# Operands of the down projection by row tiles, their remainders on VectorE, block sums moved ahead, and both halves' output projections ended token tile by token tile

## The chip, the core and the metric

The kernel runs on one NeuronCore of a Trainium2 chip. The metric is the device time of one execution in microseconds (us); lower is better. TensorE (PE) multiplies 128x128 blocks into PSUM. VectorE (DVE), ScalarE (ACT) and GpSimd (POOL) work element by element, and SyncE (SP) issues nearly all transfers between the memory outside (DRAM) and SBUF. All five run their own instruction streams and wait for each other by semaphores.

## The reference

One encoder layer on x (1024 tokens, 1024 columns, float32). Cut to what the change touches:

```python
merged = jax.nn.sigmoid(gate_a) * ya + jax.nn.sigmoid(gate_b) * yb      # two attentions before it
x = x + jnp.einsum("bsd,de->bse", merged, w_o[i])                       # output projection
h2 = rmsnorm(x, g_mlp[i])
u = jax.nn.relu(jnp.einsum("bsd,df->bsf", h2, w_up[i]))                 # 1024 -> 4096
x = x + jnp.einsum("bsf,fd->bsd", u * u, w_down[i])                     # 4096 -> 1024
h3 = rmsnorm(x, g_ple[i])
gate = jax.nn.sigmoid(jnp.einsum("bsd,de->bse", h3, w_ple_gate[i]))
x = x + gate * jnp.einsum("bsk,kd->bsd", p[i], w_ple[i])                # p: 1024 tokens, 256 columns
return rmsnorm(x, g_final)
```

The kernel keeps float32 accuracy.

## The kernel before

**A product in float32.** Each operand is split into a rounded part (fp32r, `hi`) and a remainder (`lo` = value minus `hi`), and each block product is three matmuls: hi·hi, hi·lo and lo·hi (`mm3`, L119 to L126). So each operand costs one cast (mostly ACT) and one subtraction (DVE or POOL) before PE can use it. Nearly all matmuls stand on L126.

**The stages in order.** The input projection with its gates (to about 240 us of the trace), two attentions (to 700), the merge, the output projection `wo` (766 to 861), the up projection `u` (to 1188), the down projection `d` (1188 to 1534), and the last stage: the gate product `pg`, the product `pp` of p with w_ple, and the final norm (to 1672). The 1024 tokens are worked in two halves of four tiles of 128 tokens (s).

**The order of work.** The program is written per engine as straight code. A scheduler of the framework then puts the instructions of each engine in an order, by its own model of the time; slots of a pool (a `tag` with a number of `bufs`) tie a new tile to the end of use of an older one. The order below is what it gives; each engine executes its list in that order.

**Gate stage.** For each of 16 column tiles d and for each half, `gate` loads 512 KB of w_in (`raw_g`), casts it on ACT (`hi_g`, L103), takes the remainder on DVE (`lo_g`, L105), runs 24 matmuls of 128x512 and stores the sigmoid (`gst`) to DRAM with a DMA on SP.

**Output projection.** `wo(h, n, s)` is 24 matmuls of 128x256 for the half h, the column quarter n and the token tile s. For half 0 all sixteen run first; x_rows(1, s) loads the second half, and then `upper_rows(s)` normalizes the first half's rows, sends them through a transposing DMA (`nhl` to `nt`) and leaves the transposed rows in `R`, from which the operand `H_b` is cut (L839, L840). For half 1, n = 2 and 3 already end tile by tile, and `lower_rows(s)` (L174, L864, L868, L873 to L881) normalizes and transposes on PE (`nt_mlp`) and cuts the up projection's operands `H_t`.

**Down projection.** A seven-product scheme (as Strassen's) on 2x2 blocks: four chunks c of the 4096 rows, and in each seven products i in the order 1, 2, 5, 6, 3, 7, 4 (`run`). A product has an operand from u (`ua`, read back from DRAM, 512 KB each half) and one from w_down (`wd`, in SBUF), each [128, 4, 512]; it multiplies them for four token tiles s: 48 matmuls of 128x512. It is done in two halves `sub_` of two k tiles each. `operand` (L1109 to L1113) makes [P, 2, 2, 512]: the cast on ACT (L1111, 128x1024), the remainder on POOL for `da` and on DVE for `db` (L1112, 128x1024). There are four tags, da0, db0, da1 and db1, with one buffer each, so the cast of the next product's da0 waits until PE has read this product's. Between the products `minus` (L1197, DVE) makes the sums of w_down blocks in place. Products are added to accumulators E[1] to E[7] in SBUF (`put`: L1139 ACT for the first, L1141 DVE after that).

**End of the down projection.** In the last chunk, `sums` (L1071 to L1080) combines the accumulators of half 0 into x, `norm3` (L1086 to L1092) normalizes rows into `xn` and transposes them (`nt_ple`, L202) into h3H and h3L. p is loaded, transposed on PE (`ptt`, L1101), and split into `pT` in the middle of the down projection (`p_rows`, after product 3 of chunk 1).

**Last stage.** For each half, each n of four and each s of four: `pg`, 24 matmuls of 128x256, and `pp`, six of 128x256. `quad` loads and splits w_ple_gate in two parts (`lo_pg`, POOL, L105). The sums of half 1 stand at n = 1 of half 0, and the norms of half 1's tiles 0, 1 and 2, and 3 at n = 1, 2 and 3.

## Time and profile before

| what | value |
|---|---|
| median of 3 runs | 1672.77 us (1672.07 to 1676.2) |
| the profiled execution's own time | 1674.16 us |
| its span, first to last instruction | 1672.4 us |
| TensorE busy, share of the span | 1558.0 us, 93% |
| VectorE / ScalarE / GpSimd busy | 1212.9 / 791.9 / 778.6 us |
| mean granted TensorE clock | 0.979 |

Durations and waits below come from the profiled execution, which is 1.4 us above the median. A wait of an engine costs time only where that engine's work sets the end. TensorE is busy for 93% of the span, so its waits are where a change of order can win time, and the other engines count where TensorE waits for them.

### The profile page before, as it was taken

What the parts mean: (1) busy time and instruction counts of PE and PEld (TensorE: products, weight loads), DVE (VectorE), ACT (ScalarE), POOL (GpSimd) and SP (SyncE); (2) the same over time, 40 slices, a digit from 0 to 9 for tenths busy, and PEclk for the clock granted to TensorE, in tenths of its full rate; (3) what the DMA queues carried; (4) which work ended last, traced back from release to release, by engine and by line L of the source; (5) the groups of instructions that cost most, each with busy time, mean ns of one, the idle gap of its engine ahead of it and who ended that gap; (6) DMA issues with size and microseconds to landing.
All of it is one profiled execution on the core that took longest, in us unless ns stands there. A gap on an engine that the chain in (4) does not pass through costs nothing.

```text
span 1672.4 us, 23829 instructions
## 1 busy us (share of the span) xinstructions
PE 1558.0 (93%) x8514; PEld 1319.1 (79%) x8514; DVE 1212.9 (73%) x1815; ACT 791.9 (47%) x1450; POOL 778.6 (47%) x478
## 2 busy tenths in 40 slices
PE   7999999999899887999987999999999989987978
PEld 7998887777777665789985888888787778766978
DVE  7278238668889878545588999999867767888443
ACT  6344348678898777423443222222343333333533
POOL 4254006547777778322353333333544434465743
PEclk9999999999999999999997999999999999999989
DMA  6023549979999999846634544445944443312331
GB/s 228 26 51 110 148 133 187 226 164 215 203 199 190 194 187 196 223 144 214 177 108 138 173 142 151 159 150 183 383 168 135 135 167 113 127 38 63 116 109 67
DMA packets 435814, 260.96 MB, mean 156 GB/s; under 512 B 284392, under 2 KB 381808, under 8 KB 435312
## 3 DMA queue, kind: packets, MB, share of 16 engines
q1 hardware_dynamic: 434416, 257.34, 59.3%
q10 hardware_dynamic: 1280, 2.10, 0.6%
q8 instruction: 67, 1.10, 0.3%
q14 instruction: 51, 0.42, 0.1%
HBM read 141.89 MB, written 48.30 MB: 114 GB/s over the span
## 4 chain that ended last, share of the span: by engine, by line
PE 57%; DVE 12%; DMA 11%; issue 8%; POOL 7%; ACT 4%; SPq 1%; POOLq 0%; ACTq 0%; DVEq 0%
PE u L126 17%; PE d L126 8%; PE gt L126 8%; DMA PT<-hl 7%; PE pg L126 5%; PE y L126 4%; POOL da L1112 3%; PE z_qb L126 3%; PE wo L126 3%; POOL hl L585 2%; PE av L755 2%; DVE db L1112 1%; PE z_k L126 1%; PE pp L126 1%; DVE p L574 1%
## 5 line engine op out<-in xcount | busy, mean ns | idle before, releaser
L585 POOL TENSOR_TENSOR hl<-p,hl 128x1024 f16<-128x1024 f32 x128 | 278.9, 2186 | 183.4 <-PE gt L126 69.8
L126 PE MATMUL d<-db,da 128*128 128x512 f32 x1344 | 316.7, 396 | 26.4 <-DVE db L1112 19.1
L126 PEld LDWEIGHTS d<-db,da 128*128 128x128 f32 x1344 | 255.2, 191 | 85.6 <-DVE db L1112 27.0
L1112 POOL TENSOR_TENSOR da<-ua,da 128x1024 fp32r<-128x1024 f32 x56 | 144.2, 2575 | 163.8 <-ACT da L1111 160.8
L126 PE MATMUL u<-H_t,wop 128*128 128x512 f32 x768 | 182.5, 394 | 8.5 <-ACT H_t L876 8.5
L126 PEld LDWEIGHTS u<-H_t,wop 128*128 128x128 f32 x768 | 146.1, 191 | 39.9 <-ACT H_t L876 8.9
L574 DVE TENSOR_SCALAR_CACHE_REDUCE p<-s 128x1024 f32<-128x1024 f32 x128 | 155.5, 1217 | 11.4 <-PE s L126 5.4
L1112 DVE TENSOR_TENSOR db<-wd,db 128x1024 fp32r<-128x1024 f32 x55 | 112.4, 2043 | 64.8 <-ACT db L1111 64.8
L577 ACT ACTIVATE p<-p,mx 128x1024 f32<-128x1024 f32 x128 | 147.3, 1151 | 8.9 <-DVE Va L458 1.5
L1111 ACT CAST da<-ua 128x1024 fp32r<-128x1024 f32 x56 | 58.9, 1052 | 187.6 <-issue 162.6
L126 PE MATMUL u<-H_b,wop 128*128 128x512 f32 x576 | 138.4, 394 | 4.3 <-ACT wop L798 4.3
L126 PEld LDWEIGHTS u<-H_b,wop 128*128 128x128 f32 x576 | 109.2, 190 | 27.4 <-ACT wop L798 4.7
L584 DVE TENSOR_SCALAR_CACHE_REDUCE hl<-p 128x512 f16<-128x512 f32 x128 | 87.2, 681 | 49.3 <-DMA PT<-hl 33.3
L1032 POOL TENSOR_TENSOR us<-uq 128x512 f32<-128x512 f32 x15 | 19.7, 1312 | 193.5 <-DVE uq L1028 193.5
L126 PE MATMUL s<-KT,QT 96*128 96x512 f32 x384 | 103.6, 411 | 5.8 <-DVE p L574 5.7
L126 PE MATMUL gt<-hH,hi_g 128*128 128x512 f32 x256 | 100.7, 393 | 2.6 <-ACT hi_g L103 2.6
L126 PE MATMUL gt<-hH,lo_g 128*128 128x512 f32 x256 | 101.4, 396 | 1.7 <-DVE lo_g L105 1.7
L126 PE MATMUL gt<-hL,hi_g 128*128 128x512 f32 x256 | 100.1, 391 | 0.0
L583 ACT CAST hl<-p 128x512 f16<-128x512 f32 x128 | 78.8, 616 | 26.1 <-DMA PT<-hl 23.4
L126 PEld LDWEIGHTS s<-KT,QT 96*128 96x128 f32 x384 | 70.1, 193 | 23.2 <-DVE p L574 7.5
L105 DVE TENSOR_TENSOR lo_g<-raw_g,hi_g 128x1024 fp32r<-128x1024 f32 x32 | 47.6, 1488 | 55.3 <-ACT hi_g L103 55.2
L755 PE MATMUL av<-PT,Va 128*128 128x256 f16 x512 | 66.7, 283 | 20.4 <-DMA PT<-hl 19.4
(331 smaller groups left out, 3867.3 us busy)
## 6 DMA issues: line engine op xcount, KB each, us to landing
ua<-u_d SPq DMA_DIRECT2D x56, 512.0 KB, 3.7
raw_g<-in_w_in_dram SPq DMA_DIRECT2D x32, 512.0 KB, 4.1
raw_up<-in_w_up_dram SPq DMA_DIRECT2D x32, 512.0 KB, 4.6
u_d<-us SPq DMA_DIRECT2D x64, 256.0 KB, 2.0
wd<-in_w_down_dram SPq DMA_DIRECT2D x16, 1024.0 KB, 5.8
u_d<-uq SPq DMA_DIRECT2D x48, 256.0 KB, 2.0
gates_d<-gst SPq DMA_DIRECT2D x32, 256.0 KB, 2.9
gg<-gates_d SPq DMA_DIRECT2D x16, 512.0 KB, 3.3
```

What stands on the lines that cost most here:

```text
L105: eng.tensor_tensor(lo, raw, hi.bitcast(F32), ALU.subtract)
L126: return [pe.matmul(ps, a, b, start=start and i == 0, stop=stop and i == len(m) - 1) for i, (a, b) in list(enumerate(m))[first:last]]
L574: dve.tensor_scalar(e, ps, 1.0, 3e38, op0=ALU.mult, op1=ALU.min, accum_out=mx)
L577: act.activation(e, e, AF.Exp, bias=mx, scale=-1.0, accum_out=sums[:, hd, qt:qt + 1])
L583: act.copy(hl[:, 0, :CUT], e[:, :CUT])
L584: dve.tensor_scalar(hl[:, 0, CUT:], e[:, CUT:], 1.0, 0.0, op0=ALU.mult, op1=ALU.max, accum_out=top)
L585: pool.tensor_tensor(hl[:, 1], e, hl[:, 0], ALU.subtract)
L755: pe.matmul(av[:, :256], values(hd, kt), PT[(2 * g + half) % 3][:, n, kt], start=(kt + n == 0), stop=(kt + n == NS))
L1032: eng.tensor_tensor(v[1], q[:, 2], q[:, 3], ALU.add)
L1111: act.copy(t[:, 0], raw)
L1112: eng.tensor_tensor(t[:, 1], raw, t[:, 0].bitcast(F32), ALU.subtract)
```

## The change

Six edits. (1) `p_rows` runs in the gate stage, at d = 13 and 15, and stores the transposed p to DRAM (`p_d`, eight DMAs of 128 KB through one buffer); at the end of chunk 0 of the down projection it is read back as two loads and split into `pT`. (2) In half 0 of the output projection n = 2 and 3 end tile by tile, with `upper_rows(s)` right behind each. (3) The down operands are made per k tile, [P, 2, 512], from one tag with ten buffers; PE multiplies k by k. All remainders are on DVE (except the first two of the first product), and `minus` moves to POOL. (4) The block sums are taken as soon as their parts are there: for half 0 after products 2, 6 and 3 of the last chunk, for half 1 beside the first `pg` products; `xn` of half 0 uses the storage of E[1]. (5) The product of p with w_ple for half 0, n = 0 and 1 (`pp0`), is done at the end of the down projection, as 24 matmuls of 128x512. (6) The norms of half 1 move up: tiles 0 and 1 at n = 1, 2 and 3 at n = 2.

```diff
 
+    p_d = tc.dram_tile([P, 2, S], F32, name="p_d")
...
+    def p_rows(h):
...
+        pr = raw_tile(f"p{h}", [P, 4, PLE])
+        nc.sync.dma_start(pr, p[512 * h:512 * (h + 1), :].rearrange("(s q) c -> q s c", q=P))
+        for s in range(4):
+            pt = bank(f"ptt{h}_{s}")
+            for k in range(2):
+                pe.transpose(pt[:, k * P:(k + 1) * P], pr[:, s, k * P:(k + 1) * P], ident)
+            v = pt[:, :256].rearrange("p (k s) -> p k s", k=2)
+            t = zp.tile([P, 2, P], F32, tag="junk", name=f"pt{h}_{s}", bufs=1)
+            act.copy(t, v)
+            nc.sync.dma_start(p_d[:, :, (4 * h + s) * P:(4 * h + s + 1) * P], t)
+
...
+        if d in (13, 15):
+            p_rows(d // 15)
...
-        for n in range(4):
+        for n in range(2):
             ws = wo_weights(0, n)
             for s in range(4):
                 wo(0, n, s, ws)
+        R0 = big("R0", [P, NK, 512], F32)
+        ws = [wo_weights(0, n) for n in (2, 3)]
+        for n, s in ((2, 0), (3, 0), (2, 1), (3, 1), (2, 2), (2, 3), (3, 2), (3, 3)):
+            wo(0, n, s, ws[n - 2])
+            if n == 3:
+                upper_rows(s)
...
-        R0 = big("R0", [P, NK, 512], F32)
...
-        for s in range(4):
-            upper_rows(s)
...
-         5: acc[3][:, 0], 7: acc[3][:, 1]}
+         5: acc[3][:, 0], 7: acc[3][:, 1], 8: acc[1][:, 1]}
...
 
-    def sums(h, s):
-
-        e = {i: E[i][:, s] for i in E}
-        if h == 0:
-            dve.tensor_tensor(e[2], e[2], e[1], ALU.add)
-            dve.tensor_tensor(e[6], e[6], e[1], ALU.add)
-            pool.tensor_tensor(e[3], e[3], e[5], ALU.add)
-            dve.tensor_tensor(e[3], e[3], e[6], ALU.add)
-        else:
-            x22 = acc[1][:, 1, s]
-            pool.tensor_tensor(x22, x22, e[5], ALU.add)
-            dve.tensor_tensor(e[6], e[6], e[7], ALU.add)
-            dve.tensor_tensor(x22, x22, e[6], ALU.add)
-            dve.tensor_tensor(e[4], e[4], e[6], ALU.add)
-
-    def norm3(q, h, s):
+    def add(eng, i, j, s):
+        return eng.tensor_tensor(E[i][:, s], E[i][:, s], E[j][:, s], ALU.add)
...
+    def norm3(xn, h, s):
...
-        xn = q.tile([P, D], F32, tag="xn3", name=f"xn3_{h}_{s}", bufs=2)
...
 
-    def p_rows(h):
...
-
     na, np_ = [0], [0]
     with tc.tile_pool(name="dp", bufs=1, reuse_waits="tile") as dp:
-        def operand(side, name, raw, eng):
-            t = dp.tile([P, 2, 2, 512], F32R, tag=side, name=f"{side}_{name}")
+        def operand(name, raw, eng):
+            t = dp.tile([P, 2, 512], F32R, tag="d", name=f"d{name}", bufs=10)
             act.copy(t[:, 0], raw)
             eng.tensor_tensor(t[:, 1], raw, t[:, 0].bitcast(F32), ALU.subtract)
             return t
...
 
+            def part(s, k0, k1):
+                sl = slice(s * P, (s + 1) * P)
+                mm3(pss[s], [(a[:, 0, sl], a[:, 1, sl], b[:, 0], b[:, 1]) for a, b in ab[k0:k1]],
+                    start=k0 == 0, stop=k1 == 4)
+
             ab = []
-            for sub_ in range(2):
-                ab.append((operand(f"da{sub_}", f"{i}_{c}", av[sub_], pool),
-                           operand(f"db{sub_}", f"{i}_{c}", bv[:, 2 * sub_:2 * sub_ + 2],
-                                   pool if c + sub_ == 0 and i == 1 else dve)))
+            for k in range(4):
+                eng = pool if c == 0 and i == 1 and k < 2 else dve
+                ab.append((operand(f"a{k}_{i}_{c}", av[k // 2][:, k % 2], eng), operand(f"b{k}_{i}_{c}", bv[:, k], eng)))
                 if whole:
                     continue
                 for s in range(4):
-                    if sub_ == 0:
+                    if k == 0:
                         room(s)
-                    a, b = ab[sub_]
-                    sl = slice(s * P, (s + 1) * P)
-                    mm3(pss[s], [(a[:, 0, k, sl], a[:, 1, k, sl], b[:, 0, k], b[:, 1, k]) for k in range(2)],
-                        start=sub_ == 0, stop=sub_ == 1)
-                    if sub_ == 1:
+                    part(s, k, k + 1)
+                    if k == 3:
                         put(s)
             if whole:
                 yield
                 for s in range(4):
                     room(s)
-                    sl = slice(s * P, (s + 1) * P)
-                    mm3(pss[s], [(a[:, 0, k, sl], a[:, 1, k, sl], b[:, 0, k], b[:, 1, k]) for a, b in ab for k in range(2)])
+                    part(s, 0, 4)
                     put(s)
                     yield
 
...
             def minus(o, a, b):
                 for sub_ in range(2):
                     ks = slice(2 * sub_, 2 * sub_ + 2)
-                    dve.tensor_tensor(o[:, ks], a[:, ks], b[:, ks], ALU.subtract)
+                    pool.tensor_tensor(o[:, ks], a[:, ks], b[:, ks], ALU.subtract)
                 return o
 
             run(1, c, av[0], b11)
+            t1 = minus(b11, b12, b11)
             run(2, c, av[1], b21)
-            t1 = minus(b11, b12, b11)
+            if last:
+                for s in range(4):
+                    add(pool, 2, 1, s)
+                    add(dve, 6, 1, s)
             run(5, c, av[2], t1)
             av += [a_raw(4, c)]
             t2 = minus(t1, b22, t1)
             run(6, c, av[3], t2)
             av += [a_raw(5, c)]
             t4 = minus(b21, b21, t2)
+            if last:
+                for s in range(4):
+                    add(dve, 3, 5, s)
             run(3, c, av[4], b22)
             av += [a_raw(6, c)]
             t3 = minus(b12, b22, b12)
-            if c == 1:
-                pT = big("pT", [P, 2, 2, S])
-                for h in range(2):
-                    p_rows(h)
             if last:
-                for s in range(2):
-                    sums(0, s)
+                for s in range(4):
+                    add(dve, 3, 6, s)
             run(7, c, av[5], t3)
             end = product(4, c, av[6], t4)
             if last:
                 next(end)
-                norms = []
-                for s in range(4):
-                    if s > 1:
-                        sums(0, s)
-                    norms.append(norm3(dp, 0, s))
+                x1 = E[1].rearrange("p (i s) c -> p i (s c)", i=2)
+                norms = [norm3(x1[:, s % 2], 0, s) for s in range(4)]
...
-                for t in norms[2:]:
-                    next(t)
+
+                pp0 = big("pp0", [P, 4, 512], F32)
+                wp = w_tile("wq", w_ple, 0, 2, 0, 512)
+                for s in range(4):
+                    if s % 2 == 0:
+                        next(norms[2 + s // 2])
+                    ps = bank(f"pp0_{s}")
+                    st = slice(s * P, (s + 1) * P)
+                    mm3(ps, [(pT[:, 0, k, st], pT[:, 1, k, st], wp[0][:, k], wp[1][:, k]) for k in range(2)])
+                    act.copy(pp0[:, s], ps)
             for _ in end:
                 pass
+            if c == 0:
+                pT = big("pT", [P, 2, 2, S])
+                for k in range(2):
+                    raw = raw_tile(f"pT{k}", [P, S])
+                    nc.sync.dma_start(raw, p_d[:, k])
+                    act.copy(pT[:, 0, k], raw)
+                    sub(pT[:, 1, k], raw, pT[:, 0, k])
             if not last:
                 wA = wN
 
...
         for n in range(4):
             cs = slice(256 * n, 256 * (n + 1))
             ws = quad(f"pg{h}_{n}", w_ple_gate, 256 * n, eng=pool, **({"pool_": ep, "tag": "z"} if n % 2 else {}))
-            wp = ple_weights(h, n)
+            if h > 0 or n > 1:
+                wp = ple_weights(h, n)
...
-            if h == 0 and n == 1:
-                for s in range(4):
-                    sums(1, s)
             for s in range(4):
...
                 ps = bank(f"pg{h}_{n}_{s}")
-                mm3(ps[:, :256], [(h3H[h][:, k, sl], h3L[h][:, k, sl]) + ws(k) for k in range(NK)])
-                pp = ple_product(h, n, s, wp, bank(f"pp{h}_{n}_{s}"))
+                mm = mm3(ps[:, :256], [(h3H[h][:, k, sl], h3L[h][:, k, sl]) + ws(k) for k in range(NK)])[0]
+                if h + n == 0:
+                    follow(add(dve, 6, 7, s), mm)
+                    follow(add(pool, 8, 5, s), mm)
+                    add(dve, 4, 6, s)
+                    add(dve, 8, 6, s)
+                pp = pp0[:, s, cs] if h == 0 and n < 2 else ple_product(h, n, s, wp, bank(f"pp{h}_{n}_{s}"))
...
             if h == 0 and n > 0:
-                for s in {1: (0,), 2: (1, 2), 3: (3,)}[n]:
-                    for _ in norm3(ep, 1, s):
+                for s in {1: (0, 1), 2: (2, 3), 3: ()}[n]:
+                    for _ in norm3(ep.tile([P, D], F32, tag="xn3", name=f"xn3_1_{s}"), 1, s):
...
 
```

SP in the gate stage, where the loads of weights (`raw_g`) and the stores (`gates_d`) alternate, before:

```order
L97 DMA raw_g_1_2316<-in_w_in_dram 128x8x128
L474 DMA gates_d<-gst_0_2245 128x512
L97 DMA raw_g_1_2350<-in_w_in_dram 128x8x128
L474 DMA gates_d<-gst_0_2279 128x512
L97 DMA raw_g_1_2384<-in_w_in_dram 128x8x128
L474 DMA gates_d<-gst_0_2313 128x512
```
SP at the same place with the change (`p_d` are the stores of the transposed p):

```order
L474 DMA gates_d<-gst_0_2246 128x512
L489 DMA p_d<-pt_0_2254 256x1x128
L481 DMA raw_p_2343<-in_p_dram 128x4x256
L97 DMA raw_g_1_2369<-in_w_in_dram 128x8x128
L489 DMA p_d<-pt_1_2260 256x1x128
L489 DMA p_d<-pt_2_2266 256x1x128
L474 DMA gates_d<-gst_0_2306 128x512
L97 DMA raw_g_1_2403<-in_w_in_dram 128x8x128
```
Up to two stores of p stand between a weight load and the next store of a gate, and the second load of p stands ahead of a weight load.

DVE in a chunk of the down projection (`wd` is the block of w_down, `ua` that of u, `acc` the accumulators, `d` the product in PSUM), before:

```order
L1112 TENSOR_TENSOR db_1_2_12513<-wd_0_11956,db_1_2_12513 128x1024
L1141 TENSOR_TENSOR acc_11440<-acc_11440,d_1_3_12447 128x512
L1197 TENSOR_TENSOR wd_0_11956<-wd_1_12496,wd_0_11956 128x1024
L1112 TENSOR_TENSOR db_1_2_12545<-wd_0_11956,db_1_2_12545 128x1024
L1197 TENSOR_TENSOR wd_1_12496<-wd_1_12496 128x1024
L1197 TENSOR_TENSOR wd_0_11956<-wd_1_12496,wd_0_11956 128x1024
L1197 TENSOR_TENSOR wd_1_12496<-wd_1_12496 128x1024
L1112 TENSOR_TENSOR db_2_2_12577<-wd_0_11956,db_2_2_12577 128x1024
```
DVE in a chunk with the change:

```order
L1106 TENSOR_TENSOR da_5_1_12321<-ua_1_1_12096,da_5_1_12321 128x512
L1106 TENSOR_TENSOR db_5_1_12324<-wd_0_11507,db_5_1_12324 128x512
L1135 TENSOR_TENSOR acc_11491<-acc_11491,d_1_0_12193 128x1024
L1135 TENSOR_TENSOR acc_11491<-acc_11491,d_1_2_12200 128x1024
L1106 TENSOR_TENSOR da_6_1_12349<-ua_1_0_12098,da_6_1_12349 128x512
L1106 TENSOR_TENSOR db_6_1_12352<-wd_0_11507,db_6_1_12352 128x512
L1106 TENSOR_TENSOR da_6_1_12369<-ua_1_0_12098,da_6_1_12369 128x512
L1106 TENSOR_TENSOR db_6_1_12372<-wd_0_11507,db_6_1_12372 128x512
```
The sums of `wd` are gone from DVE; both remainders, `da` and `db`, now stand there in pairs of half the size.

POOL at the end of the down projection (`lo_pg_n_j` is part j of the gate weights of quarter n, `r_ple` a factor of the norm), before:

```order
L1112 TENSOR_TENSOR da_4_3_13433<-ua_3_0_13355,da_4_3_13433 128x1024
L1112 TENSOR_TENSOR da_4_3_13439<-ua_3_1_13357,da_4_3_13439 128x1024
L105 TENSOR_TENSOR lo_pg_0_1_13617<-raw_pg_0_1_13613,hi_pg_0_1_13615 128x1024
L169 TENSOR_TENSOR r_ple_2_13490<-v_ple_2_13488,mhalf 128x1
L169 TENSOR_TENSOR r_ple_3_13540<-v_ple_3_13538,mhalf 128x1
L105 TENSOR_TENSOR lo_wp_0_13623<-raw_wp_0_13619,hi_wp_0_13621 128x512
L105 TENSOR_TENSOR lo_pg_1_0_13787<-raw_pg_1_0_13783,hi_pg_1_0_13785 128x1024
```
POOL at the same place with the change (L1088 are the block sums of half 1):

```order
L169 TENSOR_TENSOR r_ple_3_13889<-v_ple_3_13887,mhalf 128x1
L105 TENSOR_TENSOR lo_pg_1_0_14157<-raw_pg_1_0_14153,hi_pg_1_0_14155 128x1024
L1088 TENSOR_TENSOR acc_11493<-acc_11493,acc_11495 128x512 x2
L105 TENSOR_TENSOR lo_pg_1_1_14163<-raw_pg_1_1_14159,hi_pg_1_1_14161 128x1024
L1088 TENSOR_TENSOR acc_11493<-acc_11493,acc_11495 128x512
L105 TENSOR_TENSOR lo_pg_0_1_14005<-raw_pg_0_1_14001,hi_pg_0_1_14003 128x1024
L1088 TENSOR_TENSOR acc_11493<-acc_11493,acc_11495 128x512
```
The second part of the first quarter's remainder, `lo_pg_0_1`, stood ahead of both parts of the second quarter; now it stands behind them and behind three sums.

## Rows read from the trace of the kernel before

**Rows 1.** the page: busy time of each engine, share of the span, instructions

```profile
PE 1558.0 (93%) x8514; PEld 1319.1 (79%) x8514; DVE 1212.9 (73%) x1815; ACT 791.9 (47%) x1450; POOL 778.6 (47%) x478
```

**Rows 2.** windows of the four down chunks and the last stage

```profile
core 0: us, PE busy (x) PEld busy (x) DVE busy (x) ACT busy (x) POOL busy (x), PEclk, DMA share, GB/s
1187.80:1267.50 79.70, 77.13 (x338) 62.87 (x337) 55.73 (x36) 35.42 (x39) 33.37 (x14) 1.00 0.68 253
1267.50:1354.20 86.70, 80.68 (x354) 65.43 (x353) 62.21 (x53) 30.51 (x36) 34.64 (x14) 0.98 0.43 145
1354.20:1432.50 78.30, 76.79 (x338) 62.90 (x336) 62.32 (x43) 28.06 (x28) 35.01 (x15) 1.00 0.38 123
1432.50:1533.70 101.20, 84.58 (x355) 67.72 (x354) 88.61 (x78) 34.12 (x40) 58.19 (x27) 0.93 0.19 60
1533.70:1672.40 138.70, 121.82 (x1008) 120.97 (x1006) 65.43 (x127) 60.71 (x146) 70.75 (x58) 0.96 0.30 97
```

**Rows 3.** groups of TensorE in the down projection: busy, mean ns, idle before

```profile
L126 PE MATMUL d<-db,da 128*128 128x512 f32 x1344 | 316.7, 396 | 26.4 <-DVE db L1112 19.1 <-DVE pT L77 3.7 <-DVE v_ple L167 2.7
L1101 PE MATMUL ptt<-ident,raw_p 128*128 128x128 f32 x16 | 2.4, 274 | 0.3 <-DMA raw_p<-in_p_dram 0.3
```

**Rows 4.** timeline of TensorE, down: start, duration, idle before and releaser

```profile
1218.81 49.49 PE L126 MATMUL d<-db,da 128*128 128x512 f32 x217 [0.60 <-DVE db L1112]
1466.58 1.65 PE L126 MATMUL d<-db,da 128*128 128x512 f32 x3 [4.46 <-DVE db L1112]
1522.88 0.80 PE L126 MATMUL d<-db,da 128*128 128x512 f32 x1 [7.51 <-DVE db L1112]
```

**Rows 5.** a window behind one such wait, columns as in 2

```profile
1466.60:1470.00 3.40, 3.40 (x8) 2.72 (x9) 3.15 (x5) 0.00 (x0) 0.12 (x1) 0.50 0.50 150
```

**Rows 6.** timelines of VectorE, then GpSimd, in the down projection

```profile
1253.42 2.58 DVE L1112 TENSOR_TENSOR db<-wd,db 128x1024 fp32r<-128x1024 f32 x1 [2.86 <-ACT db L1111]
1267.93 1.21 DVE L1197 TENSOR_TENSOR wd<-wd,wd 128x1024 f32<-128x1024 f32 x1
1252.51 2.40 POOL L1112 TENSOR_TENSOR da<-ua,da 128x1024 fp32r<-128x1024 f32 x1 [3.04 <-ACT da L1111]
```

**Rows 7.** groups of VectorE and GpSimd, down projection

```profile
L1141 DVE TENSOR_TENSOR acc<-acc,d 128x512 f32<-128x512 f32 x47 | 30.2, 676 | 11.2 <-PE d L126 11.2
L1141 DVE TENSOR_TENSOR acc<-acc,d 128x1024 f32<-128x1024 f32 x24 | 28.5, 1207 | 0.0
L1073 POOL TENSOR_TENSOR acc<-acc,acc 128x512 f32<-128x512 f32 x4 | 6.9, 1764 | 0.0
```

**Rows 8.** groups of VectorE in the up projection

```profile
L799 DVE TENSOR_TENSOR wop<-st_s,wop 128x512 fp32r<-128x512 f32 x60 | 67.4, 1123 | 0.0
L799 DVE TENSOR_TENSOR wop<-raw_up,wop 128x512 fp32r<-128x512 f32 x43 | 29.9, 696 | 0.8 <-ACT wop L798 0.8
```

**Rows 9.** timelines, output to up projection: TensorE, then ScalarE

```profile
884.30 7.84 PE L126 MATMUL u<-H_t,wop 128*128 128x512 f32 x24 [8.48 <-ACT H_t L876]
896.42 0.79 PE L126 MATMUL u<-H_b,wop 128*128 128x512 f32 x1 [4.28 <-ACT wop L798]
848.18 1.14 ACT L839 CAST H_b<-R 128x512 fp32r<-128x512 f32 x2 [5.58 <-DVE R L855]
```

**Rows 10.** timeline of ScalarE, gate stage; a DMA of the page

```profile
225.19 1.05 ACT L103 CAST hi_g<-raw_g 128x1024 fp32r<-128x1024 f32 x1 [3.90 <-PE gt L126]
230.63 1.05 ACT L103 CAST hi_g<-raw_g 128x1024 fp32r<-128x1024 f32 x1 [3.89 <-PE gt L126]
u_d<-us SPq DMA_DIRECT2D x64, 256.0 KB, 2.0
```

**Rows 11.** timeline of TensorE in the last stage

```profile
1592.13 0.28 PE L126 MATMUL pp<-hi_wp,pT 128*128 128x256 f32 x1
1592.84 0.28 PE L126 MATMUL pg<-hi_pg,h3H 128*128 128x256 f32 x1
1605.30 1.08 PE L202 MATMUL nt_ple<-ident,xn 128*128 128x128 f32 x4 [8.74 <-DVE xn L1089]
```

More of the change, by code (lines that the diff above doesn't have):

```diff
@@ L1092, in norm3 @@
         yield
-    def p_rows(h):
-        pr = raw_tile(f"p{h}", [P, 4, PLE])
-        nc.sync.dma_start(pr, p[512 * h:512 * (h + 1), :].rearrange("(s q) c -> q s c", q=P))
-        for s in range(4):
-            pt = bank(f"ptt{h}_{s}")
-            for k in range(2):
-                pe.transpose(pt[:, k * P:(k + 1) * P], pr[:, s, k * P:(k + 1) * P], ident)
-            v = pt[:, :256].rearrange("p (k s) -> p k s", k=2)
-            sl = slice((4 * h + s) * P, (4 * h + s + 1) * P)
-            act.copy(pT[:, 0, :, sl], v)
-            sub(pT[:, 1, :, sl], v, pT[:, 0, :, sl])
     na, np_ = [0], [0]
     with tc.tile_pool(name="dp", bufs=1, reuse_waits="tile") as dp:
-        def operand(side, name, raw, eng):
-            t = dp.tile([P, 2, 2, 512], F32R, tag=side, name=f"{side}_{name}")
+        def operand(name, raw, eng):
+            t = dp.tile([P, 2, 512], F32R, tag="d", name=f"d{name}", bufs=10)
             act.copy(t[:, 0], raw)
@@ L1260, in hybrid_block_kernel @@
             ws = quad(f"pg{h}_{n}", w_ple_gate, 256 * n, eng=pool, **({"pool_": ep, "tag": "z"} if n % 2 else {}))
-            wp = ple_weights(h, n)
+            if h > 0 or n > 1:
+                wp = ple_weights(h, n)
             if gfin_b is None:
                 gfin_b = gain(ep, "gfin_b", g_final.unsqueeze(0))
-            if h == 0 and n == 1:
-                for s in range(4):
-                    sums(1, s)
             for s in range(4):
```

## The prediction

> **What bounds the kernel now.** I began with the busy times. TensorE works for 1558.0 of 1672.4 us [rows 1], so what can be won without fewer matmuls is its waits, about 114 us in all, and the slow stretches behind them. The stage windows say where: the four chunks of the down projection take 79.7, 86.7, 78.3 and 101.2 us, 345.9 together, though each multiplies the same number of matmuls, and the clock is down to 0.93 in the last [rows 2]. In a stretch without a wait TensorE starts 217 matmuls within 49.49 us, that is 49.1/216 = 0.227 us each [rows 4]. A chunk has 7 x 48 = 336 of them, 76.4 us, and the four have 305.5. So 345.9 - 305.5 = 40 us of this stage are no needed matmul time.
>
> The groups of TensorE say what ends its waits there: 26.4 us, of which 19.1 end with the remainder `db` on VectorE, 3.7 with `pT` and 2.7 with the norm [rows 3]. The two longest stand in the last chunk, 4.46 and 7.51 us [rows 4]. Each also costs something behind it: at 1466.6, right after such a wait, the granted clock is 0.50, the 1.2 GHz level, for the next 3.4 us [rows 5].
>
> Why `db` is late is read from the timelines of VectorE and GpSimd together. `da` on GpSimd begins at 1252.51 and takes 2.40 us; `db` on VectorE begins at 1253.42 and ends at 1256.00, 2.58 us after its start, though a VectorE operation of the same size without such a neighbour takes 1.21 [rows 6]. The two block each other: the second one waits for the first. In quiet products this fits into the half product that covers it (24 x 0.227 = 5.4 us), since each operand has a single buffer. When sums or norms come in between, as in the last chunk, there is no further cover, and TensorE waits.
>
> **Down operands by row tiles.** Removed: 56 `da` on GpSimd and 55 `db` on VectorE. Added on VectorE: 56 remainders of 128x512 in each chunk. An operation of this form and size takes 0.696 us for one operand of the up projection and 1.123 for another [rows 8]; I read the longer mean as the price where GpSimd runs beside it often. I take 0.70, since GpSimd now has only the eight sums of w_down blocks in a chunk: 56 x 0.70 = 39 us. Adding products to the accumulators: 30.2 + 28.5 = 58.7 us for 24 products [rows 7], 2.45 each, 17 in a chunk. Together 56 us on VectorE against 76.4 on TensorE. GpSimd's eight sums cost 8 x 2.40 = 19 us, at the price of `da` [rows 6]. If every one of them stopped VectorE for its whole length, 56 + 19 = 75 us: still just under TensorE's 76.4. Also, ten buffers hold five pairs; one pair feeds TensorE for 12 x 0.227 = 2.7 us, so up to four pairs, 10.9 us, lie ahead of it. A VectorE delay of the size seen here (7.51 at most) is then covered. So the waits for `db` go, and the half-clock stretches behind them.
>
> The Trainium skill bears on this: its page "SBUF — State Buffer", section "Who interferes with whom", says that the port pair that VectorE and GpSimd share is an exclusive lock, so that a VectorE operation with two inputs in SBUF and a GpSimd operation that reads SBUF run one after the other. The pair above agrees (1.21 alone, 2.58 beside a `da`). By the rule a chunk's VectorE and GpSimd work simply add, to the 75 us just worked out; so the rule alone doesn't deny the gain, but it leaves next to no reserve and makes the last chunk the place to look.
>
> In the last chunk come 12 VectorE and 4 GpSimd sums (12 x 0.70 = 8.4; 4 x 1.76 = 7 [rows 7]), four norm products (1.2 each, 5), four `h3L` (0.70 each, 3), and two to four remainders of gate weights on GpSimd (2.40 each, 5 to 10). VectorE 56 + 16 = 72; with GpSimd 19 + 7 + 7 = 33 the serial sum is 105 us against about 80 for TensorE. Part of it (the later sums and weights) may lie behind the last product, and most of VectorE's time need not meet GpSimd's; I take 4 us of waits, bounds 0 and 25.
>
> The sum for the stage: 305.5 for matmuls, 1.7 for 16 transposes of the norm (a `ptt` transpose of the same form is busy for 2.4/16 = 0.15 [rows 3]; 0.11 by starts is my estimate), 3 at the start of the first chunk and 1 at each of three later ones (waits of this kind as the 0.60 in [rows 4]), 4 in the last: 317. Against 345.9 that is **-29**, bounds -38 (nothing lost) and -8 (last chunk at its worst).
>
> **p moved to the gate stage.** Gone from the down projection: the `ptt` transposes and 3.7 us of wait, counted above. Added there: two loads with two remainders of 128x1024 at the end of chunk 0 (1.21 each), hidden under the four pairs. Added to the gate stage: 16 transposes, 2 us, on a TensorE that has no other slack. Each of 8 stores goes through one buffer, so ACT's next copy waits until the store before has landed. A 256 KB store lands 2.0 us after issue [rows 10]; ACT is idle for 3.90 us in each gate period of 230.63 - 225.19 = 5.44 us [rows 10]. So one such wait fits into a period, two in one don't. On SP, stores of p and the second load of p go ahead of a weight load and can hold it; that load has one spare buffer, a period. I take **+4** (2 transposes, 2 waits), bounds +2 and +12.
>
> **Output projection tile by tile.** Matmuls are the same. `upper_rows(0)` starts three groups earlier. Before, its last step still holds ACT at 848.18 after 5.58 us of waiting for `R` [rows 9], and the first statistics of `lower_rows` stand behind it; the end of that chain are TensorE's waits of 8.48 and 4.28 us [rows 9]. The chain is then VectorE's own work, which does not shrink, so not all goes: **-5**, bounds -12 and +2.
>
> **The last stage.** It takes 138.7 us [rows 2]. Norms of half 1 one quarter earlier take away the wait of 8.74 us at 1605.30 [rows 11]; what was late there is the norm on VectorE, now a quarter (11 us) ahead. Eight `pp` fewer, 1592.84 - 1592.13 = 0.71 us each [rows 11], 5.7; `pp0` adds 24 x 0.227 = 5.4, so nothing is won but cover. New: `lo_pg_0_1` stands on GpSimd behind both parts of the second quarter and three sums, 3 x 2.40 + 3 x 1.76 = 12.5 us behind `lo_pg_1_0`'s start, and that one waits for a slot that TensorE's last down matmuls free. TensorE wants it after `pp0` and the first halves of four `pg` (5.4 + 4 x 1.4 = 11 us), with transposes 12 to 13. I take a wait of 4, bounds 0 and 9. Sum: -8.7 - 0.3 + 4 = **-5**, bounds -9 and 0.
>
> **Sum.** -29 + 4 - 5 - 5 = -35 on the profiled execution's own 1674.2 (1.4 above the median of the runs): **1639 us**.
>
> **Rivals.**
> *VectorE becomes the bound.* The remainders cost what they cost beside GpSimd, 1.123 [rows 8]: 56 x 1.123 + 17 = 80 us in a chunk, 3.6 above TensorE, and the last chunk at the upper bound. The stage is then 4 x 80 + 3 + 15 = 338 instead of 317: 1660. For it: VectorE and GpSimd block each other in every product now [rows 6]. Against: GpSimd has 19 us in a chunk where `da` had 14 x 2.40 = 34.
> *The wait moves into the last stage.* `lo_pg_0_1` comes 9 or more late and the clock halves behind it, as in [rows 5]: nothing is won there (5 more), and the slow stretch costs 2: 1646. For it: the order shown. Against: that wait has only one place.
> *Slower.* In the gate stage each of the eight stores costs a full gate period, since ACT's copy, the cast of the next weights and SP's next load stand behind it in turn: 8 x 5.44 = 43.5 instead of 4, 1639 + 39.5 = 1679. It decides from the point at which a copy waits longer than ACT's 3.90 us [rows 10]. For it: one buffer for all. Against: 2.0 us to landing for twice the size.
>
> **How the numbers follow.** Forecast 0.62, its own range 1626 to 1650; VectorE as the bound 0.16; the moved wait 0.11; slower 0.06; 0.05 for gains that fail in several places. The range 1620 to 1662 holds the first three cases nearly whole. A measurement of this kernel can tell 0.3%, 5 us, from no change: faster 0.91, same 0.03, slower 0.06.
>
> **What would show it.** Right: chunks of 77 to 79 us and a last one below 90, no wait of TensorE on a remainder above 2 us before it, no `ptt` in the down projection, and the wait at the norm gone from the last stage. VectorE as the bound would show as VectorE busy above 95% of a chunk with remainders near 1.1 us. Wrong: gates that follow each other at over 5.44 us around the stores, or a last chunk of 100 us as before.

## The result, and the profile after

The change made the kernel slower: median 1693.45 us (1690.63 to 1694.6, 4 runs) against 1674.49 us (1672.07 to 1677.68, 4 runs) for the kernel before beside it. The ratio is 1.011, 95% interval 1.0089 to 1.013. The profiled execution took 1694.5 us, its span 1692.7.

The windows of the down projection and the last stage, columns as in [rows 2]; the first is the stretch between the last matmul of the up projection and the first of the down projection:

```profile
1206.80:1235.50 28.70, 0.39 (x2) 0.00 (x0) 3.73 (x6) 0.64 (x2) 0.00 (x0) 0.56 0.94 371
1235.50:1314.70 79.20, 79.03 (x337) 64.77 (x338) 63.72 (x67) 44.66 (x76) 31.79 (x13) 0.97 0.41 140
1314.70:1390.80 76.10, 76.10 (x337) 63.03 (x336) 62.12 (x77) 32.01 (x56) 20.56 (x8) 1.00 0.45 153
1390.80:1467.00 76.20, 76.20 (x338) 63.08 (x337) 63.10 (x79) 32.00 (x56) 20.57 (x8) 1.00 0.38 125
1467.00:1552.90 85.90, 79.74 (x355) 65.98 (x354) 78.78 (x98) 36.49 (x63) 31.32 (x16) 0.96 0.21 68
1552.90:1692.70 139.80, 123.88 (x984) 121.22 (x982) 82.96 (x137) 60.95 (x148) 77.42 (x61) 0.96 0.28 95
```

The chunks of 79.7, 86.7, 78.3 and 101.2 us [rows 2] are now 79.2, 76.1, 76.2 and 85.9, and two of them have no wait at all. But ahead of them stand 28.7 us in which TensorE does next to nothing, and the last stage is no shorter. What is left in the last chunk is one long wait, on the norm and not on a remainder:

```profile
1538.59 0.69 PE L202 MATMUL nt_ple<-ident,acc 128*128 128x128 f32 x2 [6.16 <-DVE acc L1096]
```

The timelines at the wait ahead of the down projection, TensorE, ScalarE and SP's queue (start, duration, idle before and what ended it):

```profile
1235.53 2.15 PE L126 MATMUL d<-db,da 128*128 128x512 f32 x3 [28.34 <-ACT db L1105]
...
1196.88 0.61 ACT L1105 CAST da<-ua 128x512 fp32r<-128x512 f32 x1
1234.86 0.62 ACT L1105 CAST db<-wd 128x512 fp32r<-128x512 f32 x1 [37.36 <-DMA u_d<-us]
...
1207.86 4.87 SPq L980 DMA_DIRECT2D wd<-in_w_down_dram  x2
1212.78 6.67 SPq L986 DMA_DIRECT2D ua<-u_d  x1
1221.32 3.12 SPq L1057 DMA_DIRECT2D u_d<-us  x3
1228.33 0.32 SPq L1057 DMA_DIRECT2D u_d<-us  x1
```

The first operand is cast at 1196.88, before the up projection ends. The second waits 37.36 us, and not for its weights: it waits for `u_d<-us`, the last store of the up projection's results, which SP issues at 1228.33, behind loads of the next operands. The cast doesn't read `us`. In the built program its tile, [128, 2, 512] of the ring, lies at bytes 218944 to 223040 of each partition (a partition is one of the 128 rows of SBUF), and there lay `us2` and `us3`, the staging tiles of the up projection's last results, until then. The four single buffers of the kernel before took 182080 to 214848; ten buffers of 4 KB reach to 223040. The 8 KB between were in use before as well, but by two `xn` tiles that are first written in the last chunk, when those stores have long landed. The built program of the changed kernel already has this: that cast waits for six DMA queues, VectorE and GpSimd.

The gate stage, ScalarE and SP:

```profile
204.21 1.05 ACT L103 CAST hi_g<-raw_g 128x1024 fp32r<-128x1024 f32 x1 [5.45 <-DMA raw_g<-in_w_in_dram]
210.64 1.04 ACT L103 CAST hi_g<-raw_g 128x1024 fp32r<-128x1024 f32 x1 [4.38 <-DMA raw_g<-in_w_in_dram]
212.08 0.36 ACT L488 COPY pt<-ptt 128x256 f32<-128x256 f32 x1
216.50 0.37 ACT L488 COPY pt<-ptt 128x256 f32<-128x256 f32 x1 [4.05 <-DMA p_d<-pt]
221.90 1.05 ACT L103 CAST hi_g<-raw_g 128x1024 fp32r<-128x1024 f32 x1 [5.03 <-DMA raw_g<-in_w_in_dram]
...
212.60 0.59 SPq L489 DMA_DIRECT2D p_d<-pt  x1
216.90 6.86 SPq L489 DMA_DIRECT2D p_d<-pt  x2
...
212.24 0.44 PE L485 MATMUL ptt<-ident,raw_p 128*128 128x128 f32 x2 [2.77 <-ACT gst L473]
230.70 0.69 PE L485 MATMUL ptt<-ident,raw_p 128*128 128x128 f32 x2 [4.38 <-ACT gst L473]
```

A copy waits 4.05 us for the landing of the store before it, the next cast of weights comes 11.26 us after the last (210.64) where the period was 5.44 [rows 10], and TensorE waits for ScalarE to empty a PSUM bank.

The first of these waits of TensorE (2.77) has another origin than the stores. The casts at 204.21 and 210.64 already wait for weights, and the second comes 6.43 us after the first, ahead of the first copy of p. In the built program p is loaded into one of the two `raw` tiles that the weights take turns in; while p lies there, two sets of weights in a row (`raw_g14`, `raw_g15`) use the other tile, and the second is loaded only when the first has been read.

Of the 12.7 us lost in this stage, 2.77 + 4.38 = 7.2 are these two waits and 2 the transposes of p. The granted clock was 0.93, 0.90 and 0.83 in the three windows of 10 us from 205 to 235; from that I estimate the rest at 0.7 + 1.0 + 1.7 = 3.4 us.

The two waits at the start of the up projection, and the remainders on VectorE, are:

```profile
904.33 8.33 PE L126 MATMUL u<-H_t,wop 128*128 128x512 f32 x24 [8.29 <-ACT H_t L893]
917.02 1.22 PE L126 MATMUL u<-H_b,wop 128*128 128x512 f32 x2 [4.35 <-ACT wop L815]
...
L1106 DVE TENSOR_TENSOR db<-wd,db 128x512 fp32r<-128x512 f32 x110 | 113.5, 1032 | 0.0
L1106 DVE TENSOR_TENSOR da<-ua,da 128x512 fp32r<-128x512 f32 x110 | 92.6, 842 | 61.9 <-ACT da L1105 61.9
```

The two waits were 8.48 and 4.28 [rows 9]. Last, who TensorE waits for in the last stage, first before, then after (in all, times, longest):

```profile
PE nt_ple L202 <- DVE xn L1089: 8.7, 1, 8.7
PE pg L126 <- DVE h3L L77: 0.9, 2, 0.6
```
```profile
PE pg L126 <- ACT sg L1286: 3.1, 2, 2.7
PE pg L126 <- DVE h3L L77: 3.1, 2, 2.4
PE nt_ple L202 <- ACT sg L1286: 1.5, 1, 1.5
PE pg L126 <- POOL lo_pg L105: 1.2, 1, 1.2
```

9.6 us of waits became 8.9, at other places.

Where each kernel stands at the same marks of its profiled execution (us, starts of matmuls in TensorE's timeline; the last five columns are experiments below, norm_back is ring8_p_norm_back):

| first or last matmul | before | after | ring8 | ring8_p_back | before_ring8 | norm_back | best |
|---|---|---|---|---|---|---|---|
| first of attention (s) | 243.9 | 256.6 | 256.6 | 243.7 | 244.0 | 243.7 | 243.6 |
| first behind attention (y) | 668.7 | 687.7 | 682.7 | 670.1 | 666.2 | 668.1 | 665.8 |
| first of up | 861.5 | 883.2 | 879.7 | 862.1 | 858.1 | 861.6 | 858.2 |
| last of up | 1187.6 | 1206.8 | 1203.7 | 1187.3 | 1184.3 | 1185.4 | 1183.2 |
| first of down | 1187.8 | 1235.5 | 1203.9 | 1187.5 | 1184.5 | 1185.6 | 1183.4 |
| last of down | 1533.3 | 1552.5 | 1523.5 | 1510.7 | 1511.5 | 1507.9 | 1505.3 |
| last of pg | 1664.1 | 1684.7 | 1656.0 | 1643.5 | 1643.8 | 1646.2 | 1636.1 |

Against the kernel before, the changed one is 12.7 us late at the first matmul of attention, 19.2 at the end of the up projection, 47.7 at the start of the down projection, 19.2 again at its end, and 20.6 at the last `pg`. So the down projection itself won 28.5 us, and the wait ahead of it lost them.

### The profile page after: what moved, and what is told of

The parts are those of the page before. It is cut to its first block, busy times and chain, and to the rows that moved or that the text cites. A ratio compares the mean times of both kernels' runs of the same rounds, so it can differ in the third digit from the quotient of the medians.

```text
span 1692.7 us, 24069 instructions
## 1 busy us (share of the span) xinstructions
PE 1559.0 (92%) x8490; PEld 1319.3 (78%) x8490; DVE 1231.8 (73%) x1943; ACT 810.3 (48%) x1567; POOL 726.5 (43%) x455
## 4 chain that ended last, share of the span: by engine, by line
PE 48%; DMA 13%; DVE 10%; issue 5%; ACT 5%; POOL 2%; SPq 0%; POOLq 0%; ACTq 0%; DVEq 0%
PE u L126 17%; PE d L126 15%; DMA PT<-hl 6%; PE y L126 4%; PE pg L126 3%; PE wo L126 2%; PE av L772 2%; POOL hl L602 2%; ACT p L594 1%; DMA wd<-in_w_down_dram 1%; PE gt L126 1%; ACT hl L600 1%; DVE p L591 1%; DMA bc<-rs_d 1%; DVE acc L1088 1%
## 5 line engine op out<-in xcount | busy, mean ns | idle before, releaser
L126 PE MATMUL d<-db,da 128*128 128x512 f32 x1344 | 308.8, 392 | 28.5 <-ACT db L1105 28.3
L1105 ACT CAST da<-ua 128x512 fp32r<-128x512 f32 x112 | 69.7, 623 | 146.0 <-PE d L126 143.5
L1106 DVE TENSOR_TENSOR da<-ua,da 128x512 fp32r<-128x512 f32 x110 | 92.6, 842 | 61.9 <-ACT da L1105 61.9
L601 DVE TENSOR_SCALAR_CACHE_REDUCE hl<-p 128x512 f16<-128x512 f32 x128 | 87.2, 681 | 55.7 <-DMA PT<-hl 39.4
L1191 POOL TENSOR_TENSOR wd<-wd,wd 128x1024 f32<-128x1024 f32 x16 | 41.2, 2578 | 170.9 <-DVE db L1106 169.0
L1106 DVE TENSOR_TENSOR db<-wd,db 128x512 fp32r<-128x512 f32 x110 | 113.5, 1032 | 0.0
```

What stands on the lines that cost most here:

```text
L126: return [pe.matmul(ps, a, b, start=start and i == 0, stop=stop and i == len(m) - 1) for i, (a, b) in list(enumerate(m))[first:last]]
L601: dve.tensor_scalar(hl[:, 0, CUT:], e[:, CUT:], 1.0, 0.0, op0=ALU.mult, op1=ALU.max, accum_out=top)
L1105: act.copy(t[:, 0], raw)
L1106: eng.tensor_tensor(t[:, 1], raw, t[:, 0].bitcast(F32), ALU.subtract)
L1191: pool.tensor_tensor(o[:, ks], a[:, ks], b[:, ks], ALU.subtract)
```

## The experiments

Times are medians; the ratio and its 95% interval are against the kernel before that ran beside the experiment. Its median was 1671.92 in the first four; 1675.11 beside ring8_p_wo_back, ring8_p_da_pool, ring8_p_lo_dve and ring8_pt_pairs; 1674.76 beside before_ring8, ring8_p_norm_back, best and ring8_pt_dve; 1674.85 beside the last two. Medians from different groups are therefore not compared to better than 3 us; the ratios and the marks above are. Theory at the start: the wait at the down projection comes from where the ring lies in memory, and the 12.7 us of the gate stage from the stores of p. Rivals: late transfers of the first operands; a cause of its own in attention.

**ring8.**

```diff
-            t = dp.tile([P, 2, 512], F32R, tag="d", name=f"d{name}", bufs=10)
+            t = dp.tile([P, 2, 512], F32R, tag="d", name=f"d{name}", bufs=8)
```

> The changed kernel with 8 instead of 10 operand buffers. Theory (memory of the ring): ten buffers of 4 KB reach into the 10 KB where the up projection's last staging tiles lie, and the second operand cast waits until their stores have landed; eight end just below. Then the 28.3 us wait at the start of the down projection shrinks to 0 to 4, the rest stays: 1665 to 1670 us. Rival (transfers): the first operands themselves come late on SP's queue; then the wait stays at 26 to 30 and the time at 1690 to 1695.

Measured: 1663.74 us, ratio 0.9952 (0.9932 to 0.9972), 1.3 below the expected range. Against the change (1.011) that is 1.6% or 26 us; the medians differ by 29.7, but by the marks, too, the stretch from the last of up to the last of down is 26 us shorter (345.7 and 319.8). The first `db` cast, and below it the same in ring9:

```profile
1199.39 0.62 ACT L1105 CAST db<-wd 128x512 fp32r<-128x512 f32 x1 [5.02 <-DVE uq L1021]
```
```profile
1229.09 0.62 ACT L1105 CAST db<-wd 128x512 fp32r<-128x512 f32 x1 [34.84 <-DMA u_d<-uq]
```

With eight the second operand waits for VectorE, which reads the tile there last, and the store no longer comes into it: in the built program this cast waits for one DMA queue and VectorE. The stores themselves are issued in the same order behind the same loads as with ten. The transfers' rival is gone. Eight buffers of 4 KB are no more memory than the four of 8 KB before.

**ring9.** `bufs=9`.

> The changed kernel with 9 operand buffers. By the memory theory the second cast now overlaps only the staging tiles that are stored first, so the wait lasts until the first of the last stores has landed: 18 to 25 us instead of 28.3, time 1685 to 1690. By the transfer rival nothing changes: 28, 1690 to 1695.

Measured: 1695.54 us, 1.0147 (1.0114 to 1.0181). The wait was 25.8 us, ended by a store that SP issued one place before the one that ended it with ten. The direction held, the size did not (18 to 25 expected), and the time missed: the last chunk took 91 us, 5 more than with ten. Why was not tried.

**p_back.** `p_rows` stands in chunk 1 of the down projection again, writes `pT` from PSUM, and nothing of p goes through DRAM.

```diff
-        if d in (13, 15):
-            p_rows(d // 15)
...
+            if c == 1:
+                pT = big("pT", [P, 2, 2, S])
+                for h in range(2):
+                    p_rows(h)
```

> The changed kernel with the rows of p transposed in chunk 1 of the down projection again, nothing of it in the gate stage. Theory (stores through one buffer hold the gate loads): the first attention matmul comes 12 to 13 us earlier, near 244, and the 6 us that attention then lost on top go too, since their only source is the shifted start; some 4 us come back in the down projection: 1678 to 1684 us. Rival: attention's 6 us have another cause and stay: 1684 to 1688.

Measured: 1675.88 us, 1.0016 (1.0001 to 1.0032), 2 below the expected range. The first matmul of attention is at 243.6. Attention took 426.3 us, 4.7 less than in the changed kernel; but in ring8, where p is as in the change, it took 426.1, so this does not hang on p. The wait at the down projection is still there (27.8). In the down projection p costs 78.1 - 76.2 = 1.9 us in chunk 1: with the ring as cover, nothing but its transposes.

**ring8_p_back.** Both.

> Both of these together. If the two costs are separate they add: 1693 - 25 - 13 (or 9 to 15) = 1652 to 1662 us, below the kernel before by 13 to 22. If one hides behind the other: above 1665.

Measured: 1651.35 us, 0.9876 (0.9852 to 0.9899), 0.7 below the expected range. The first four experiments share a kernel before, so their medians can be compared: the ring taken back to eight wins 24.5 us (p_back to here), and p taken back 12.4 (ring8 to here). So neither hides behind the other. Counted from the changed kernel's median, ring8 and p_back win 29.7 and 17.6, 5 more than the 42.1 together. Attention took 431 us in the changed kernel's profiled execution and 426 in each of these three, with the same instructions; that is counted in both and would account for the 5.

**ring8_p_wo_back.** From ring8_p_back, with half 0 in its old order: all sixteen `wo`, then `upper_rows`.

```diff
-        for n in range(2):
+        for n in range(4):
...
+        for s in range(4):
+            upper_rows(s)
```

> Eight buffers, p in the down projection, and half 0's output projection in the old order with upper_rows after it. The prediction's step (tile by tile wins 5 us): slower by 5 than the 1651.4 of the same kernel with the new order. Theory now (TensorE's waits of 9.1 and 5.0 us at the start of the up projection are there in either order, because VectorE's queue sets them): 1649 to 1653 us, waits of 8 to 9 and 4 to 5 as before.

Measured: 1649.26 us, 0.9849 (0.9821 to 0.9876), not slower than with the new order. The same two waits in ring8_p_back, then here:

```profile
883.58 8.01 PE L126 MATMUL u<-H_t,wop 128*128 128x512 f32 x24 [8.67 <-ACT H_t L876]
896.24 1.22 PE L126 MATMUL u<-H_b,wop 128*128 128x512 f32 x2 [4.64 <-ACT wop L798]
```
```profile
882.80 7.65 PE L126 MATMUL u<-H_t,wop 128*128 128x512 f32 x24 [8.48 <-ACT H_t L876]
894.73 0.79 PE L126 MATMUL u<-H_b,wop 128*128 128x512 f32 x1 [4.28 <-ACT wop L798]
```

**ring8_p_da_pool.** Who makes the remainders: `da` and the sums of w_down go back to the engines of before, tiles and ring stay.

```diff
-operand(f"a{k}_{i}_{c}", av[k // 2][:, k % 2], eng)
+operand(f"a{k}_{i}_{c}", av[k // 2][:, k % 2], pool)
...
-                    pool.tensor_tensor(o[:, ks], a[:, ks], b[:, ks], ALU.subtract)
+                    dve.tensor_tensor(o[:, ks], a[:, ks], b[:, ks], ALU.subtract)
```

> Eight buffers, p in the down projection, but the remainders da on GpSimd and the sums of w_down on VectorE again, so that only the row tiles and the ring are left of the change to the operands. Theory A (the ring covers late remainders, whoever makes them): chunks of 78 to 80 us still, 1650 to 1656 us. Theory B (moving the remainders off GpSimd is what counts, since the two engines block each other): half of the 23 us of the stage come back, 1660 to 1668 us.

Measured: 1653.44 us, 0.9875 (0.9846 to 0.9904). The chunk windows:

```profile
1182.90:1268.60 85.70, 80.06 (x338) 65.20 (x337) 61.48 (x50) 41.68 (x72) 45.00 (x31) 0.96 0.65 240
1268.60:1346.60 78.00, 78.00 (x354) 64.63 (x353) 62.14 (x64) 34.26 (x64) 39.08 (x28) 1.00 0.46 154
1346.60:1422.80 76.20, 76.20 (x338) 63.10 (x337) 62.57 (x60) 31.96 (x56) 40.14 (x29) 1.00 0.41 133
1422.80:1510.90 88.10, 82.00 (x353) 66.73 (x352) 82.40 (x81) 37.11 (x65) 51.70 (x34) 0.96 0.21 66
```

Theory A holds: remainders still take longer than alone (`db` 1.165 us on VectorE beside `da` of 1.464 on GpSimd, where 0.696 was the shorter mean in [rows 8]), and yet three chunks are as short as in ring8_p_back (78.1, 77.1 and 87.4). Only the first is 5 us longer (80.8 there). The finer tiles and the ring stand in this run together; none has one without the other.

**ring8_p_lo_dve.** `eng=dve if h + n == 0 else pool` for the gate weights.

> Eight buffers, p in the down projection, and the remainder of the first quarter's gate weights on VectorE. Theory (lo_pg_0_1 is late because it stands on GpSimd behind the second quarter's parts and the sums): TensorE's wait of 4.3 us on it goes, 1645 to 1649 us. Rival (the wait only changes its name, since h3L or the weights' load is as late): 1650 to 1653.

Measured: 1647.87 us, 0.9841 (0.9811 to 0.9871), within the theory's range, but not for its reason. The wait on `lo_pg` (4.3 in ring8_p_back) is gone, and this is what TensorE waits for then:

```profile
PE pg L126 <- ACT sg L1279: 3.2, 2, 2.6
PE nt_ple L202 <- ACT sg L1279: 3.0, 2, 1.5
PE pg L126 <- DVE h3L L77: 2.6, 2, 2.0
```

8.8 us instead of 9.4; from the last `d` to the last `pg` it takes as long as before the edit (132.6 and 132.8 by the marks). In the profiled executions the gain lies in attention (421.0 us against 426.5), which the edit does not touch. So the rival was right about the last stage.

**before_ring8.** The third edit alone on the kernel before, with eight buffers: `operand`, `part`, the loop over k and `minus` on GpSimd, as in the change; everything else as before.

> The kernel before with the third edit alone: down operands by row tiles, eight buffers in one ring, remainders on VectorE, the sums of w_down on GpSimd; block sums, norms, p, output projection and last stage as before. Theory (the ring is what wins): the down projection takes 322 to 328 us instead of 345.5, 1650 to 1656 us. Rival (the early block sums and the norms of edit 4 are needed for the last chunk): last chunk still 95 to 101, 1658 to 1664.

Measured: 1653.51 us, 0.9877 (0.9846 to 0.9909). One edit of six, with eight buffers, gives 21 us beside its kernel before; all of them without the two losses (ring8_p_back) gave 20.6 beside theirs. The last chunk (91.3) is 4 us longer than with the early sums (87.2); the last stage still has its wait of 8.7.

**ring8_p_norm_back.** The norms of half 1 at their old places.

```diff
-                for s in {1: (0, 1), 2: (2, 3), 3: ()}[n]:
+                for s in {1: (0,), 2: (1, 2), 3: (3,)}[n]:
```

> Eight buffers, p in the down projection, and the norms of half 1 at their old places (tile 0 at the second quarter, 1 and 2 at the third, 3 at the fourth). The prediction's step (moving them up takes away 8.7 us of wait): 1657 to 1660 against 1651.4, with one wait of 8 to 9 us at a norm. Theory now (VectorE's work of norms, sums and gate products is the same, so the wait is only cut into pieces): TensorE's waits in the last stage stay at 9 to 11 us in all, 1649 to 1654.

Measured: 1656.95 us, 0.9896 (0.9866 to 0.9925). The ratios alone do not tell it from ring8_p_back (0.9876, up to 0.9899), but by the marks the stretch from the last `d` to the last `pg` is 5.5 us longer (138.3 and 132.8), and the wait is back:

```profile
1586.86 1.51 PE L202 MATMUL nt_ple<-ident,xn 128*128 128x128 f32 x6 [8.74 <-DVE xn L1079]
```

My theory fell: the wait comes back at its old size, on top of the new ones (16.0 us in all). Moving the norms does take it away; the other edits of the last stage add waits of about the same sum.

**ring8_pt_pairs, ring8_pt_dve, ring8_pt_poolq, ring8_pt_dve_poolq.** What in the gate stage costs 12.7 us, all with eight buffers and p in the gate stage. Pairs: two token tiles in one tile of 256 KB, four stores. dve: `dve.tensor_copy(t, v)` for `act.copy(t, v)`. poolq: `nc.gpsimd.dma_start` for the stores.

> Eight buffers, p still in the gate stage, but stored in four pieces of 256 KB instead of eight of 128 KB through the same one buffer: half as many copies have to wait for a landing. Theory (each landing holds ScalarE and with it the weights): the first attention matmul comes at 248 to 251 instead of 256.6, 1656 to 1660 us against 1663.7. Rival (the stores' places on SP's queue are what delays the weight loads): still 255 to 257, 1662 to 1665.

> Eight buffers, p in the gate stage with its eight stores, but the copies out of PSUM on VectorE, which has the most idle time there. Theory (a copy that waits for the landing of the store before holds ScalarE's casts of weights): the first attention matmul comes at 246 to 250 instead of 256.6, 1653 to 1658. Rival (what holds the weights is SP's queue, where the stores wait in order ahead of the loads): still 253 to 258, 1660 to 1666.

> Eight buffers, p in the gate stage, copies on ScalarE as in the change, but the eight stores issued from GpSimd's queue instead of SP's (GpSimd does nothing in that stretch). If SP's queue, in which the stores waited ahead of the weight loads, is the larger part of what is left: first attention matmul at 246 to 250 against 256.6. If ScalarE, held by copies that wait for a landing, is the larger part: 253 to 256.

> The same with the copies on VectorE as well, so that neither ScalarE nor SP waits for a landing. If these two are the whole cause, only the transposes on TensorE are left: first attention matmul at 245 to 247, 2 us behind the kernel before, 1651 to 1655 us. If it stays above 249, something else, such as the PSUM buffers of the transposes or the slot of the loaded p, holds the gates as well.

| | ring8 | pairs | dve | poolq | dve and poolq |
|---|---|---|---|---|---|
| first of attention | 256.6 | 254.5 | 251.6 | 259.2 | 251.2 |
| median | 1663.74 | 1664.62 | 1657.73 | 1666.83 | 1656.45 |

Pairs missed its theory (248 to 251): fewer stores, but one of 256 KB held its copy 6.11 us. dve came later than expected (246 to 250) but with its time within the range; poolq lies outside both of its ranges; and dve_poolq stays above 249, so something else holds the gates as well. SP's queue is not the cause: without the stores on it nothing is won (259.2, and 251.2 against 251.6). In poolq, ScalarE shows why:

```profile
232.38 0.37 ACT L488 COPY pt<-ptt 128x256 f32<-128x256 f32 x1 [4.19 <-DMA p_d<-pt]
235.32 0.37 ACT L488 COPY pt<-ptt 128x256 f32<-128x256 f32 x1 [2.57 <-DMA p_d<-pt]
238.28 0.37 ACT L488 COPY pt<-ptt 128x256 f32<-128x256 f32 x1 [2.58 <-DMA p_d<-pt]
241.23 0.37 ACT L488 COPY pt<-ptt 128x256 f32<-128x256 f32 x1 [2.58 <-DMA p_d<-pt]
241.50 1.05 ACT L103 CAST hi_g<-raw_g 128x1024 fp32r<-128x1024 f32 x1
```

Four copies stand in a row, each waits for a landing, and the cast of the next weights stands behind them all. Off ScalarE that part goes, 5 to 8 us. Some 7 us stay with copies and stores both elsewhere. The transposes are 2 of them, and TensorE waits three times, 1.68, 1.04 and 0.32 us, each time for a bank that ScalarE or VectorE empties:

```profile
211.75 0.74 PE L126 MATMUL gt<-hH,hi_g 128*128 128x512 f32 x1 [1.68 <-ACT gst L473]
...
205.00:215.00 10.00, 8.24 (x33) 6.37 (x32) 3.34 (x4) 2.37 (x4) 0.82 (x1) 0.84 0.65 184
```

The second row is a window with a granted clock of 0.84, which I estimate at 1.6 us of 10. Transposes, waits and clock make 6.6 of the 7.5 us. The wait of 1.68 stands where 2.77 stood in the changed kernel, and all four runs load p into the weights' tile. No run loads it elsewhere, so what that costs by itself is not shown.

**best.** From ring8_p_lo_dve, with half 0 in its old order.

> A version to beat both: eight buffers, p in the down projection, the old order of the output projection, and the remainder of the first quarter's gate weights on VectorE. What the runs so far give: 1651.4 - 0 to 2 (order) - 0 to 3 (gate weights) = 1646 to 1651 us, 23 to 28 below the kernel before.

Measured: 1648.25 us (1644.39 to 1652.81, 5 runs), 0.9845 (0.9818 to 0.9872): 26 us below the kernel before and 45 below the changed one. It is not told apart from ring8_p_lo_dve (1647.87) or ring8_p_wo_back (1649.26).

## Why the prediction was wrong

**The step that failed: "3 at the start of the first chunk".** It measured 28.3 us. The prediction took the ring for cover only, counted its buffers and not where they lie, and looked at no wait on memory that another stage still uses. ring8 shows this to be the cause: the wait goes, and the ratio falls from 1.011 to 0.9952. (What is left at the start with eight buffers, waits of 1.76, 1.03 and 0.38 us, is what the 3 stood for.) Between the forecast of 1639 and the 1694.5 of the profiled execution lie 55 us: 29 here, 9 in the gate stage, 5 for the output projection, 6 in the last stage, and 6.5 more between the first matmul of attention and the last of up, which the forecast did not have. The signs that the prediction named as right nearly all came true, chunks, norm and `ptt`: they looked inside the stages, and the largest loss stood between two of them. One of its signs of being wrong came true as well, gates more than 5.44 us apart around the stores.

**The down operands, -29.** Right, once it begins: 345.5 us became 316.9 from first to last matmul, with no further wait in the first chunk; in ring8, without that wait, 319.6. The reason given was half right. What counts is the row tiles with the ring (ring8_p_da_pool), not who makes the remainders; and a remainder cost 0.84 and 1.03 us in the mean, not the 0.70 taken, since GpSimd still stands in the way:

```profile
1332.97 2.73 POOL L1191 TENSOR_TENSOR wd<-wd 128x1024 f32<-128x1024 f32 x1
1333.37 2.89 DVE L1106 TENSOR_TENSOR db<-wd,db 128x512 fp32r<-128x512 f32 x1
1336.18 0.68 DVE L1106 TENSOR_TENSOR da<-ua,da 128x512 fp32r<-128x512 f32 x1
```

The Trainium skill's page "SBUF — State Buffer", section "Who interferes with whom", says that a VectorE operation with two inputs in SBUF and a GpSimd operation that reads SBUF exclude each other. These rows agree (2.89 beside a GpSimd sum, 0.68 without one), and the chunks of 76.1 and 76.2 us without a wait show that a reserve of a few tiles makes it harmless here. The last chunk's long wait was 6.2 (4 taken). The rival that makes VectorE the bound did not come about: it was busy for 62.1 and 63.1 us of the chunks of 76.1 and 76.2.

**p in the gate stage, +4.** Mis-sized: 12.7, just past the upper bound of 12. I took two waits for a landing at 2.0 us each, from a row of another store; ScalarE waited four times, 4.05, 1.73, 2.52 and 1.72 us, and the casts and activations behind these copies came late in turn. And "that load has one spare buffer" was wrong: p itself takes the spare buffer, and TensorE's first wait in the stage stands behind that. The clock after the two waits was not in the sum. The rival that made the change slower had the mechanism of the copies, but at 43.5 us it was far too dear, and by itself it does not make the change slower: ring8 keeps it and is at 0.9952.

**The output projection, -5.** Nothing, as ring8_p_wo_back shows. The step said that not all of the two waits goes; none of it went. The chain of `lower_rows` is VectorE's own work: in the 22 us behind the output projection it is busy for 21.9 in ring8_p_back (862 to 884) and for 22.9 of 23 in ring8_p_wo_back (860 to 883). And the output projection takes as long from its first to its last matmul in either order, 94.5 and 94.2 us.

**The last stage, -5.** +1. The wait at the norm went (ring8_p_norm_back), as forecast; new waits were put at 4 us on `lo_pg`, and the waits left were 8.9, most of them on the sigmoid and on h3L; the wait on `lo_pg`, which a rival put at 9 or more, was 1.2. That `lo_pg` alone is removed without gain (ring8_p_lo_dve) suggests that the stretch has several waits of about the same end.

**The rest of the 19 us at the end of the up projection** was not forecast, and its cause stays open. From the first matmul of attention to the first behind it, the changed kernel took 431.0 us and before 424.8; the other kernels, with the same attention, took 421.0 to 426.5 in their profiled executions, ring8 with the same instructions as the change 426.1. So most of this is probably not the change's. The granted clock does not set that execution apart (0.965 over the stretch, and 0.960 in ring8_p_back, which took 426.5). Another 2.5 us are waits of TensorE on `lo_wo` in the output projection; ring8 has them too, p_back has 0.3, so they come with p in the gate stage. How was not tried.
